# Products of the modulation moved ahead, sums kept in PSUM, and the first and last blocks of the feed-forward part reordered, in a one-core diffusion block

## The chip, the cores and the metric

The kernel runs on one core of a Trainium2 chip. The metric is the device time of one execution in microseconds (us). In the code and the views PE is TensorE, PEld its weight loads, DVE is VectorE, ACT ScalarE, POOL GpSimd and SP SyncE, whose queue issues most DMAs.

## The reference

One layer of a block over 1024 latent tokens (a 16 by 64 grid) of width 1024, with 256 context tokens beside. Cut to what matters:

```python
sh1, sc1, g1, sh2, sc2, g2 = split(silu(c) @ mod_w + mod_b, 6)
h = rms_norm(x, norm1_g) * (1 + sc1) + sh1
z_f, z_x, z_y, z_g = split(h @ w_in)                # 512 | 1024 | 1024 | 2 x 1024
f = real(fft2(z_f, per group of 128, ortho)) @ w_fourier
r = (lru_scans(z_x) * gelu(z_y)) @ w_lru_out
g_f, g_r = split(sigmoid(z_g))
x = x + g1 * ((g_f * f + g_r * r) @ w_o)
h2 = rms_norm(x, norm2_g) * (1 + sc2) + sh2
gate, val = split(dwconv3x3(h2 @ ffn_w_up), 2)      # 2 x 2816 channels
x = x + g2 * ((gelu(gate) * val) @ ffn_w_down)
return rms_norm(x, final_g)
```

All is fp32.

## The kernel before

Every matrix product is made in three: each fp32 operand is split into a high part (a copy rounded to fp32r, mostly by ScalarE, L131) and a low part (the difference, by VectorE or GpSimd, L138), and TensorE adds high x high, high x low and low x high in PSUM (`mm3`, L183 to L194). So each operand needs two instructions on other engines before TensorE can read it. Buffers in SBUF are slots of 4 KB per partition, handed out first in, first out by an allocator (`Slots`): a tile that gets a slot, and the DMA that fills it, waits until the last use of the slot before is over. No scheduler reorders anything: each engine runs its instructions in the order of the Python code, and several queues of thunks (`between` lists, `tasks`, `todo`) place the work of one chain between the matmuls of another.

The stages, with their time in the profile:

- To 370: norm, context, input projections, the two scans of the recurrence.
- `lru_out` (L855), 370 to 494: for j = 4 to 11, 48 matmuls into one bank pair, then the product with the gate (L885). Weights are loaded and split ahead by `use`.
- `fourier` (L922), 494 to 696. `fold` (L893) makes sums and differences of a channel block on GpSimd (L899) and VectorE (L903 to L913). `transform` (L947) and `project` (L962) are the two matmul steps on the folded data. `gate(j)` (L984) runs 48 matmuls of the gate's projection and calls the thunks of its `between` list after the matmul numbers given there. `merge` (L1215) joins even and odd parts of block j from PSUM, multiplies by the gate `sf[j]` and adds `self.m[j]`, the recurrent branch.
- `out_proj` (L1276), 696 to 785. `post` (L1295) multiplies by the g1 row and adds the residual.
- `ffn` (L1627), 785 to 1268: 22 blocks n of 256 channels. A block is seven products i = 0 to 6 (`up_product`, L1545, 12 matmuls each), in the manner of Strassen; `up_split` makes the parts of a product's weights (ScalarE and GpSimd), `up_join` (L1571) adds the last term on VectorE to the bank of gate ("g") or value ("v"), `up_conv` prepares the 3x3 convolution, and `taps` (L1606) does its taps on VectorE. L1661 adds two side columns on GpSimd, which value's taps need.
- `down` (L1796), 1268 to the end: seven products p, in the order 1, 2, 6, 7, 5, 4, 3, of 11 steps i of 12 matmuls. `down_sums` (L1743), `down_hi`, `down_lo` make the operands; `tasks` holds the work on finished banks, two tasks a step. Rows come out in eight tiles of 128: tiles 4 to 7 are normed by `norm` (L1825) from `tasks`, tiles 0 to 3 after the last product.

The modulation rows are made aside: `mod` (L328) multiplies 128 rows of `mod_w`, loaded by SyncE (L349), by a column of silu(c) and adds them up on VectorE (L336 for the first of eight, L338 for the others), 32 products in the order shift 2, scale 2, g1, g2. `mod_finish` (L352) counts down and then sums over the partitions, for shift and scale by transposes on TensorE (L431) and a reduction on VectorE (L432).

```python
L876  if j == 11 and i % 6 == 5:
L877      sl.free(ph[i // 6], pl[i // 6])
L878      if i == 5 or i > 20:
L879          self.mod(2 if i == 5 else 3)
L1223 nc.vector.tensor_tensor(f[:, 0:H], od, e, op=OP.add)        # od: PSUM
L1225 nc.vector.tensor_tensor(f, f, sf[j], op=OP.mult)
L1226 nc.vector.tensor_tensor(f, self.m[j], f, op=OP.add)
```

Of the kernel before, what the change touches and what calls it, by code (L numbers as in the profile page):

```python
# [112 lines left out]
class K:  # L113
# [741 lines left out]
    def lru_out(self):  # L855
# [66 lines left out]
    def fourier(self):  # L922
# [146 lines left out]
        for j in range(1, 5):  # L1069
# [3 lines left out]
            if j < 4:  # L1073
                at += [*((i, self.mod) for i in (4, 13, 22, 31, 40)),
# [201 lines left out]
    def out_proj(self):  # L1276
# [197 lines left out]
        for kp in range(4):  # L1474
            low("T3", kp, st[kp][:, 0], "pool")
            sl.free(st.pop(kp))
            if kp == 1:
                self.up_split(0, 5)
        for kp in range(4):
            low("T4", kp, f0[kp][:, 1], "pool")  # L1480
            sl.free(f0.pop(kp))
# [145 lines left out]
    def ffn(self):  # L1627
# [4 lines left out]
        todo = deque([(0, 6), (1, 4), (1, 5), (1, 6)])  # L1632
        self.down_plan()
        for n in range(NP):
# [4 lines left out]
            for m, i in [(n, 0), (n - 1, 6)] + [(n, i) for i in range(1, 6)]:  # L1639
                if m >= 0 and not (n < 2 and (i < 4 and m == n or n == 0 and i == 4)):  # L1640
                    if todo:
                        self.up_split(*todo.popleft())
# [395 lines left out]
```

## Time and profile before

| | |
|---|---|
| time, median of 3 runs | 1506.07 us (1505.95 to 1506.21) |
| profiled execution, its own time | 1508.81 us |
| its span, first to last instruction | 1507.0 us |
| mean granted TensorE clock | 0.972 of full speed |
| TensorE busy | 1397.0 us (93%), 6333 matmuls |
| VectorE busy | 1146.8 us (76%), 1330 instructions |
| ScalarE busy | 694.1 us (46%) |
| GpSimd busy | 642.3 us (43%) |
| chain that ended last, by engine | PE 39%, DVE 10%, POOL 3%, issue 3% |
| bytes moved | 155.21 MB, 103 GB/s |

TensorE is the busiest engine, and its share is the mean over stages of different kinds. The profile is read by stage: where TensorE is busy less than the whole stretch, its waits name the engine and the line that released it. A wait is put down to what came last. A granted clock below 1.00 tells that matmuls of that stretch took longer for the same work. Times in a timeline count from the start of the span.

### The profile page before, as it was taken

To read this page: it belongs to the slowest core of one execution; us is meant where nothing else is said; L and a number is where in the kernel's file an instruction comes from. 1 tells how busy PE (TensorE), PEld (TensorE's weight loads), DVE (VectorE), ACT (ScalarE), POOL (GpSimd) and SP (SyncE) were. 2 spreads that over 40 slices of the span, in tenths; PEclk is the share of its full clock that TensorE was granted. 3 is DMA by queue.
4 is the path that set the end of the run, shared out by engine and by line. 5 is a ranking of instruction groups with operands and counts; after the bars stand their busy time and mean duration, and the time that the engine had idled before them with its cause. 6 is when DMAs were issued, how large, how long until landed. Compare 5 with 4: busy or idle time off the path is not lost.

```text
span 1507.0 us, 17062 instructions
## 1 busy us (share of the span) xinstructions
PE 1397.0 (93%) x6333; PEld 1126.6 (75%) x6333; DVE 1146.8 (76%) x1330; ACT 694.1 (46%) x1006; POOL 642.3 (43%) x460
## 2 busy tenths in 40 slices
PE   5999999998999689988998699999999999999994
PEld 3788888877888578877876477777777777788883
DVE  5768768767113987577566699999999998998696
ACT  6566677755010112343235355545545555545461
POOL 2221121122001443268033999999999996200000
PEclk9999999999999899999998799999999999999997
DMA  9310110101113445322431122122222108741642
GB/s 373 110 36 22 50 35 22 63 28 42 43 48 114 168 147 168 122 85 83 140 112 53 32 85 73 62 76 85 84 84 84 62 37 315 292 147 57 234 136 112
DMA packets 52788, 155.21 MB, mean 103 GB/s; under 512 B 5781, under 2 KB 10192, under 8 KB 52704
## 3 DMA queue, kind: packets, MB, share of 16 engines
q1 hardware_dynamic: 51264, 151.76, 29.0%
q10 hardware_dynamic: 1184, 2.11, 0.5%
q8 instruction: 50, 0.82, 0.2%
q14 instruction: 34, 0.28, 0.1%
q0 software_dynamic: 256, 0.25, 0.1%
HBM read 131.29 MB, written 22.81 MB: 102 GB/s over the span
## 4 chain that ended last, share of the span: by engine, by line
PE 39%; DVE 10%; POOL 3%; issue 3%; ACT 2%; DMA 1%; POOLq 0%; SPq 0%; DVEq 0%; ACTq 0%
PE ug L1556 16%; PE uv L1556 12%; PE dn L1836 6%; PE big L194 5%; DVE s L138 3%; POOL s L138 2%; ACT uv L131 1%; DVE s L1225 1%; DVE s L1828 1%; DMA s<-G 1%; ACT s L131 1%; DVE s L1757 0%; PE big L1212 0%; DVE s L1754 0%; ACT s L1341 0%
## 5 line engine op out<-in xcount | busy, mean ns | idle before, releaser
L194 PE MATMUL big<-s,s 128*128 128x512 f32 (+2 forms) x2352 | 561.5, 397 | 8.4 <-DVE s L138 5.6
L194 PEld LDWEIGHTS big<-s,s 128*128 128x128 f32 (+2 forms) x2352 | 440.4, 190 | 114.7 <-DVE s L138 7.0
L138 POOL TENSOR_TENSOR s<-s,s 128x512 fp32r<-128x512 f32 (+1 forms) x225 | 341.5, 1536 | 206.9 <-ACT s L131 132.0
L131 ACT ACTIVATE s<-s 128x512 fp32r<-128x512 f32 (+2 forms) x406 | 266.3, 698 | 237.4 <-DVE mid L912 62.8
L1556 PE MATMUL ug<-s,s 128*128 128x512 f32 x1056 | 264.4, 398 | 17.5 <-ACT uv L131 13.4
L1556 PEld LDWEIGHTS ug<-s,s 128*128 128x128 f32 x1056 | 198.1, 189 | 72.2 <-ACT uv L131 22.0
L138 DVE TENSOR_TENSOR s<-s,s 128x512 fp32r<-128x512 f32 (+3 forms) x213 | 189.9, 923 | 75.1 <-ACT s L131 53.7
L1606 DVE SCALAR_TENSOR_TENSOR s<-ug,rest,s 128x945 f32<-128x945 f32 (+2 forms) x176 | 215.0, 1221 | 9.2 <-ACT s L1585 3.8
L1836 PE MATMUL dn<-s,s 128*128 128x512 f32 x924 | 216.5, 396 | 4.2 <-DVE s L138 4.1
L1556 PE MATMUL uv<-s,s 128*128 128x512 f32 x792 | 202.1, 404 | 17.6 <-POOL s L138 6.7
L1836 PEld LDWEIGHTS dn<-s,s 128*128 128x128 f32 x924 | 174.2, 189 | 46.2 <-DVE s L138 5.7
L1606 DVE SCALAR_TENSOR_TENSOR s<-uv,rest,s 128x945 f32<-128x945 f32 (+2 forms) x155 | 189.5, 1223 | 13.5 <-POOL s L1661 9.6
L1556 PEld LDWEIGHTS uv<-s,s 128*128 128x128 f32 x792 | 152.9, 194 | 55.8 <-POOL s L138 7.9
L782 POOL TENSOR_TENSOR s<-s,s 128x1280 f32<-128x1280 f32 x8 | 25.2, 3150 | 190.1 <-ACT s L778 190.1
L899 POOL TENSOR_TENSOR s<-s,s 128x1024 f32<-128x1024 f32 x8 | 22.2, 2780 | 126.2 <-PE big L194 120.6
L131 ACT ACTIVATE p<-uv 128x512 f32<-128x512 f32 x22 | 13.2, 599 | 103.5 <-PE uv L1556 99.8
L745 DVE SCALAR_TENSOR_TENSOR s<-big,par,s 128x1023 f32<-128x1023 f32 (+1 forms) x24 | 30.8, 1282 | 34.2 <-ACT s L742 33.6
L885 DVE TENSOR_TENSOR s<-big,s 128x1024 f32<-128x1024 f32 x8 | 9.8, 1223 | 61.1 <-PE big L194 61.1
L1504 POOL TENSOR_TENSOR s<-s,s 128x512 f32<-128x512 f32 x22 | 28.5, 1295 | 64.6 <-DMA s<-in_ffn_w_up_b_dram 64.6
L1661 POOL TENSOR_TENSOR s<-s,m 128x504 f32<-128x504 f32 (+1 forms) x42 | 45.5, 1104 | 23.7 <-ACT m L1602 23.7
L1616 POOL TENSOR_TENSOR s<-s,s 128x1024 f32<-128x1024 f32 x22 | 53.7, 2440 | 2.9 <-DVE s L1606 2.9
L777 ACT ACTIVATE s<-big,rest 128x1024 f32<-128x1024 f32 x32 | 35.7, 1117 | 24.7 <-PE big L194 17.8
(233 smaller groups left out, 1500.4 us busy)
## 6 DMA issues: line engine op xcount, KB each, us to landing
s<-in_mod_w_dram SPq DMA_DIRECT2D x48, 512.0 KB, 4.6
s<-in_ffn_w_up_b_dram SPq DMA_DIRECT2D x44, 512.0 KB, 4.2
s<-in_w_in_b_dram SPq DMA_DIRECT2D x32, 512.0 KB, 4.4
s<-G SPq DMA_DIRECT2D x55, 256.0 KB, 3.9
G<-s SPq DMA_DIRECT2D x22, 512.0 KB, 2.6
s<-in_ffn_w_down_dram SPq DMA_DIRECT2D x22, 512.0 KB, 7.3
s<-in_x_dram SPq DMA_DIRECT2D x16, 512.0 KB, 5.3
s<-G SPq DMA_DIRECT2D x11, 512.0 KB, 8.4
```

What stands on the lines that cost most here:

```text
L131: self.nc.scalar.activation(out, in_, AF.Copy)
L138: (self.nc.vector if eng == "dve" else self.nc.gpsimd).tensor_tensor(out, a, b, op=OP.subtract)
L194: return [lambda x=x: nc.tensor.matmul(x[0], x[1], x[2], start=x[3], stop=x[4]) for x in calls]
L745: nc.vector.scalar_tensor_tensor(u[:, lo:hi], z[:, lo + s:hi + s], tap[t], u[:, lo:hi], op0=OP.mult, op1=OP.add)
L777: nc.scalar.activation(lat, ps, AF.Sigmoid, bias=col)
L782: nc.gpsimd.tensor_tensor(i, i, u, op=OP.mult)
L1504: p.tensor_tensor(u["x"][:, L], rg[:, L], rv[:, L], op=OP.subtract)
L1556: nc.tensor.matmul(o, x, y, start=first, stop=k == 3 and m == 2, skip_group_check=not fresh)
L1606: nc.vector.scalar_tensor_tensor(o, i, w, o, op0=OP.mult, op1=OP.add))
L1616: nc.gpsimd.tensor_tensor(u["ga"], u["ga"], u["va"], op=OP.mult)
L1661: self.nc.gpsimd.tensor_tensor(o, o, m, op=OP.add)
L1836: nc.tensor.matmul(bank[j], x, z, start=first and m == 0, stop=end and m == 2, skip_group_check=not check)
```

## The change

1. `lru_out`: for j = 4 to 10 `mod(1)` is called after matmuls 5, 21 and 37, and `mod_finish` after each matmul from j = 5 on; at j = 11 one call of `mod` is left. In the Fourier stage `gate(0)` makes no call any more, and the gates 1 to 3 make two each, not five.
2. `merge`: the copy, difference, sum and product are written to the PSUM tile itself, and only the last addition writes SBUF. In `post` of `out_proj` the product is written in place too.
3. The FFN's start: the lows of "T4" are made earlier, the splits of (0,5), (1,4), (0,6) come directly behind those of "T3", and the three products run one after the other; then value's join and convolution of block 0, and then the splits of (1,5) and (1,6).
4. `down`: right halves of the second weight rows are multiplied by the g2 row before product 3. The residual of tiles 0 to 3, with what is already known of the right half, is copied by ScalarE into the banks X, and product 3 adds onto it. Tiles 4 to 7 are normed together behind the last lows; tiles 0 to 3 are normed by pairs, in half rows, each half with its own output DMA.

```diff
@@ lru_out
                     f()
+                    if j < 11 and i in (5, 21, 37):
+                        self.mod(1)
+                    if j > 4:
+                        self.mod_finish()
                     if j == 11 and i % 6 == 5:
                         sl.free(ph[i // 6], pl[i // 6])
-                        if i == 5 or i > 20:
-                            self.mod(2 if i == 5 else 3)
+                        if i == 5:
+                            self.mod(2)
@@ fourier
-        gate(0, [(8, lambda: step(1, 2)), (17, lambda: transform(0)), (20, lambda: step(1)), (34, lambda: transform(1)),
-                 *((i, self.mod) for i in (0, 3, 24, 32, 41))])
+        gate(0, [(8, lambda: step(1, 2)), (17, lambda: transform(0)), (20, lambda: step(1)), (34, lambda: transform(1))])
@@
-                at += [*((i, self.mod) for i in (4, 13, 22, 31, 40)),
+                at += [*((i, self.mod) for i in (22, 40)),
@@ merge
-            nc.vector.tensor_copy(f[:, H:H + 1], eb[:, Q:Q + 1])
-            nc.vector.tensor_tensor(f[:, 0:H], od, e, op=OP.add)
-            nc.vector.tensor_tensor(rev(f[:, H + 1:]), e[:, 1:], od[:, 1:], op=OP.subtract)
-            nc.vector.tensor_tensor(f, f, sf[j], op=OP.mult)
-            nc.vector.tensor_tensor(f, self.m[j], f, op=OP.add)
+            nc.vector.tensor_copy(ps[:, H:H + 1], eb[:, Q:Q + 1])
+            nc.vector.tensor_tensor(rev(ps[:, H + 1:]), e[:, 1:], od[:, 1:], op=OP.subtract)
+            nc.vector.tensor_tensor(od, od, e, op=OP.add)
+            nc.vector.tensor_tensor(ps, ps, sf[j], op=OP.mult)
+            nc.vector.tensor_tensor(f, ps, self.m[j], op=OP.add)
@@ ffn
-        todo = deque([(0, 6), (1, 4), (1, 5), (1, 6)])
+        todo = deque([(1, 5), (1, 6)])
@@
+                if n == 0 and i == 5:
+                    self.up_product(0, 5)
+                    self.up_product(1, 4)
+                    self.up_product(0, 6)
+                    self.taps(0, "gt", 8)
+                    self.up_join(0, "v")
+                    self.up_conv(0, "v")
+                    while todo:
+                        self.up_split(*todo.popleft())
+                elif m > 0 and not (n == 1 and i < 5):
@@ down_sums, p == 3
             v.tensor_tensor(x[:, L], x[:, L], x[:, R], op=OP.subtract)
+            v.tensor_tensor(o[:, R], o[:, R], self.g2row[:, R], op=OP.mult)
@@ down, p == 3 and i == 7
+                    v.tensor_tensor(ss[:, 4:8], q[:, 4:8, 0], q[:, 4:8, 1], op=OP.add)
+                    r47 = self.rstd(ss[:, 4:8])()
                     for j in range(4):
...
+                        norm(4 + j, r47[:, j:j + 1])
@@ down, tasks of p == 5
-                    def c1(j=j):
-                        v.tensor_tensor(y[j][:, H[0]], y[j][:, H[0]], c11[j], op=OP.add)
+                    def c1(j=j, b=X[j]):
                         v.tensor_tensor(y[j][:, H[1]], y[j][:, H[1]], at(u, j), op=OP.add)
-                        square(j, 0, j)
+                        self.copy("act", b, y[j][:, H[1]])
@@ down, end
-                v.tensor_tensor(r, X[j], self.g2row[:, H[1]], op=OP.mult)
-                v.tensor_tensor(y[j][:, H[1]], y[j][:, H[1]], r, op=OP.add)
-                square(j, 1, j)
-            if j:
-                norm(j - 1)
+            nc.scalar.activation(temp(j), X[j], AF.Square, accum_out=sq[:, 2 * j + 1:2 * j + 2])
+            if j % 2:
+                v.tensor_tensor(ss[:, j - 1:j + 1], q[:, j - 1:j + 1, 0], q[:, j - 1:j + 1, 1], op=OP.add)
+                r = self.rstd(ss[:, j - 1:j + 1])()
+                for t in (j - 1, j):
+                    for d, x in ((1, X[t]), (0, y[t][:, H[0]])):
+                        v.scalar_tensor_tensor(y[t][:, H[d]], x, r[:, t - j + 1:t - j + 2], fg[:, H[d]], op0=OP.mult, op1=OP.mult)
```

VectorE in `lru_out`, blocks j = 5 to 7, before: a block's product with its gate (L885), then the lows of the coming weights (L138).

```order
L885 TENSOR_TENSOR s_2458<-big,s_2458 128x1024
L138 TENSOR_TENSOR s_2909<-s_2856,s_2908 128x1024
L138 TENSOR_TENSOR s_2966<-s_2912,s_2965 128x1024
L885 TENSOR_TENSOR s_2597<-big,s_2597 128x1024
L138 TENSOR_TENSOR s_3022<-s_2969,s_3021 128x1024
L138 TENSOR_TENSOR s_3079<-s_3025,s_3078 128x1024
L885 TENSOR_TENSOR s_2648<-big,s_2648 128x1024
```

Between two L885 stand two lows and nothing else. The same place with the change (L885 is now L889):

```order
L338 SCALAR_TENSOR_TENSOR s_2752<-s_2790,s,s_2752 128x1024
L338 SCALAR_TENSOR_TENSOR s_2752<-s_2874,s,s_2752 128x1024
L338 SCALAR_TENSOR_TENSOR s_2752<-s_2893,s,s_2752 128x1024
L889 TENSOR_TENSOR s_2458<-big,s_2458 128x1024
L138 TENSOR_TENSOR s_2926<-s_2864,s_2925 128x1024
L138 TENSOR_TENSOR s_2983<-s_2929,s_2982 128x1024
L338 SCALAR_TENSOR_TENSOR s_2752<-s_2912,s,s_2752 128x1024
L338 SCALAR_TENSOR_TENSOR s_2752<-s_2996,s,s_2752 128x1024
L338 SCALAR_TENSOR_TENSOR s_2752<-s_3015,s,s_2752 128x1024
L889 TENSOR_TENSOR s_2597<-big,s_2597 128x1024
```

Two or three products of the modulation now stand behind each block's lows and ahead of the next block's L889.

GpSimd at the FFN's start, before: lows (L138), the sums for block 2 (L1504 to L1508), and the two side columns (L1661).

```order
L138 TENSOR_TENSOR s_5761<-s_5354,s_5760 128x512
L138 TENSOR_TENSOR s_5761<-s_5371,s_5760 128x512
L138 TENSOR_TENSOR s_5908<-s_5501,s_5908 128x512
L1504 TENSOR_TENSOR s_5938<-s_5904,s_5906 128x512
L1506 TENSOR_TENSOR s_5906<-s_5906 128x512
L1508 TENSOR_TENSOR s_5938<-s_5906,s_5938 128x512
L138 TENSOR_TENSOR s_5942<-s_5904,s_5942 128x512
L138 TENSOR_TENSOR s_5945<-s_5539,s_5945 128x512
L138 TENSOR_TENSOR s_5960<-s_5906,s_5960 128x512
L1661 TENSOR_TENSOR s_5963<-s_5963,m 128x8x63
L1661 TENSOR_TENSOR s_5963<-s_5963,m 128x7x63
```

Behind the lows of (0,6) (s_5908) come the sums, three lows and the side columns. With the change (L1507 to L1511 are the sums, L1672 the side columns; s_5868, s_5871 and s_5874 are lows of (0,5), (1,4) and (0,6), s_5967 and s_5970 those of (1,5) and (1,6)):

```order
L138 TENSOR_TENSOR s_5868<-s_5509,s_5868 128x512
L138 TENSOR_TENSOR s_5871<-s_5539,s_5871 128x512
L138 TENSOR_TENSOR s_5874<-s_5501,s_5874 128x512
L138 TENSOR_TENSOR s_5967<-s_5561,s_5967 128x512
L138 TENSOR_TENSOR s_5970<-s_5541,s_5970 128x512
L1507 TENSOR_TENSOR s_5977<-s_5910,s_5912 128x512
L1509 TENSOR_TENSOR s_5912<-s_5912 128x512
L1511 TENSOR_TENSOR s_5977<-s_5912,s_5977 128x512
L138 TENSOR_TENSOR s_5981<-s_5910,s_5981 128x512
L138 TENSOR_TENSOR s_5984<-s_5912,s_5984 128x512
L1672 TENSOR_TENSOR s_5961<-s_5961,m 128x8x63
L1672 TENSOR_TENSOR s_5961<-s_5961,m 128x7x63
```

The three splits now stand one behind the other, and the lows of (1,5) and (1,6) moved in front of the sums, so that seven steps stand between the low of (0,6) and the side columns.

VectorE ahead of the last matmuls, before: two norms of tiles 4 to 7 (L1828 ends one), then the last two lows (L138).

```order
L1828 SCALAR_TENSOR_TENSOR s_10396<-s_10396,r_10800,s_10340 128x1024
L1826 TENSOR_SCALAR ss_9091<-sq 128x1
L453 TENSOR_SCALAR ss_9091<-ss_9091 128x1
L454 RECIPROCAL r_10811<-t_10812 128x1
L456 TENSOR_SCALAR t_10812<-r_10811,ss_9091 128x1
L457 TENSOR_SCALAR t_10812<-t_10812 128x1
L458 TENSOR_SCALAR r_10811<-r_10811,t_10812 128x1
L1828 SCALAR_TENSOR_TENSOR s_10422<-s_10422,r_10811,s_10340 128x1024
L138 TENSOR_TENSOR s_10793<-s_10748,s_10793 128x512
L138 TENSOR_TENSOR s_10794<-s_9484,s_10794 128x512
```

The lows stand last. With the change (L1890 to L463 are the small steps for four tiles at once, L1837 the scalings):

```order
L138 TENSOR_TENSOR s_10786<-s_10761,s_10786 128x512
L138 TENSOR_TENSOR s_10787<-s_9484,s_10787 128x512
L1890 TENSOR_TENSOR ss_9091<-sq 128x4
L453 TENSOR_SCALAR ss_9091<-ss_9091 128x4
L454 RECIPROCAL r_10807<-t_10808 128x4
L460 TENSOR_TENSOR t_10808<-r_10807 128x4
L461 TENSOR_TENSOR t_10808<-t_10808,ss_9091 128x4
L462 TENSOR_SCALAR t_10808<-t_10808 128x4
L463 TENSOR_TENSOR r_10807<-r_10807,t_10808 128x4
L1837 SCALAR_TENSOR_TENSOR s_10357<-s_10357,r_10807,s_10348 128x1024
```

The last lows now stand ahead of all norms.

## Rows read from the trace of the kernel before

**Rows 1.** Busy time by stage: us, then each engine busy (instructions), PEclk, DMA share, GB/s.

```profile
370.00:494.00 124.00, 124.00 (x531) 100.21 (x530) 29.23 (x22) 12.77 (x13) 6.00 (x2) 0.99 0.25 80
494.00:532.00 38.00, 26.56 (x121) 22.20 (x120) 36.12 (x61) 7.83 (x12) 18.50 (x7) 0.78 0.39 134
...
655.00:696.00 41.00, 31.95 (x164) 26.97 (x163) 40.14 (x37) 18.36 (x34) 35.04 (x15) 0.88 0.13 39
...
1480.00:1491.00 11.00, 10.57 (x38) 8.19 (x38) 4.78 (x11) 1.63 (x5) 0.00 (x0) 0.84 0.08 34
```

**Rows 2.** Timeline of TensorE, Fourier blocks: start, us, operation [idle before <-releaser].

```profile
513.04 1.09 PE L431 MATMUL sm<-ident,s 128*128 128x128 f32 x4 [7.83 <-DVE s L338]
...
515.63 4.93 PE L979 MATMUL big<-s,s 128*128 128x256 f32 x28
...
542.97 3.05 PE L979 MATMUL big<-s,s 128*128 128x256 f32 x24
...
570.24 3.04 PE L979 MATMUL big<-s,s 128*128 128x256 f32 x24
...
589.39 3.08 PE L979 MATMUL big<-s,s 128*128 128x256 f32 x24
```

**Rows 3.** Groups of instructions of VectorE, 494 to 700: busy, mean ns, idle before.

```profile
L338 DVE SCALAR_TENSOR_TENSOR s<-s,s,s 128x1024 f32<-128x1024 f32 x25 | 38.6, 1544 | 0.4
```

**Rows 4.** Groups of instructions of VectorE, 370 to 490.

```profile
L138 DVE TENSOR_TENSOR s<-s,s 128x1024 fp32r<-128x1024 f32 x10 | 12.2, 1219 | 32.3 <-ACT s L131 21.5 <-issue 10.8
L885 DVE TENSOR_TENSOR s<-big,s 128x1024 f32<-128x1024 f32 x7 | 8.6, 1225 | 61.1 <-PE big L194 61.1
```

**Rows 5.** DMA issues of the page: count, KB each, us to landing.

```profile
s<-in_mod_w_dram SPq DMA_DIRECT2D x48, 512.0 KB, 4.6
```

**Rows 6.** Waits of TensorE, 490 to 710: us in total, times, longest.

```profile
PE big L1212 <- DVE s L1224: 8.3, 4, 3.1
```

**Rows 7.** Groups of instructions of VectorE, 494 to 700, the merges.

```profile
L1225 DVE TENSOR_TENSOR s<-s,s 128x1024 f32<-128x1024 f32 x7 | 15.5, 2209 | 0.2
L1226 DVE TENSOR_TENSOR s<-s,s 128x1024 f32<-128x1024 f32 x7 | 14.6, 2086 | 0.2
...
L1223 DVE TENSOR_TENSOR s<-big,even 128x512 f32<-128x512 f32 x7 | 4.7, 677 | 0.0
```

**Rows 8.** Timeline of VectorE, first FFN blocks.

```profile
823.10 0.70 DVE L1574 TENSOR_TENSOR ug<-ug,p 128x512 f32<-128x512 f32 x1 [4.38 <-PE ug L1556]
...
847.82 6.29 DVE L1606 SCALAR_TENSOR_TENSOR s<-uv,rest,s 128x960 f32<-128x960 f32 x5 [9.55 <-POOL s L1661]
```

**Rows 9.** Timeline of TensorE, first FFN blocks.

```profile
828.17 1.22 PE L1556 MATMUL uv<-s,s 128*128 128x512 f32 x2 [5.18 <-ACT s L131]
...
838.32 5.21 PE L1556 MATMUL uv<-s,s 128*128 128x512 f32 x12 [4.69 <-DVE uv L1574]
...
855.35 4.64 PE L1556 MATMUL uv<-s,s 128*128 128x512 f32 x10 [6.58 <-POOL s L138]
...
862.72 2.92 PE L1556 MATMUL uv<-s,s 128*128 128x512 f32 x12
```

**Rows 10.** Timeline of GpSimd, first FFN blocks.

```profile
838.09 1.28 POOL L1504 TENSOR_TENSOR s<-s,s 128x512 f32<-128x512 f32 x1
...
845.62 2.17 POOL L1661 TENSOR_TENSOR s<-s,m 128x504 f32<-128x504 f32 x2
```

**Rows 11.** Timeline of TensorE, the end.

```profile
1480.00 10.57 PE L1836 MATMUL dn<-s,s 128*128 128x512 f32 x38 [3.33 <-DVE s L138]
```

**Rows 12.** Timeline of VectorE, the end.

```profile
1478.66 1.29 DVE L138 TENSOR_TENSOR s<-s,s 128x512 fp32r<-128x512 f32 x2
...
1489.89 1.28 DVE L1828 SCALAR_TENSOR_TENSOR s<-s,r,s 128x1024 f32<-128x1024 f32 x1
...
1494.54 1.29 DVE L1828 SCALAR_TENSOR_TENSOR s<-s,r,s 128x1024 f32<-128x1024 f32 x1
...
1501.97 1.28 DVE L1828 SCALAR_TENSOR_TENSOR s<-s,r,s 128x1024 f32<-128x1024 f32 x1
```

More of the change, by code (lines that the diff above doesn't have):

```diff
@@ L1296, in post @@
             n = xn[t] = sl.get([128, 1024], any_=True)
-            nc.vector.tensor_tensor(n, ps, self.g1row, op=OP.mult)
-            nc.vector.tensor_tensor(x[t], n, x[t], op=OP.add)
+            nc.vector.tensor_tensor(ps, ps, self.g1row, op=OP.mult)
+            nc.vector.tensor_tensor(x[t], ps, x[t], op=OP.add)
             nc.scalar.activation(n, x[t], AF.Square, accum_out=ss[:, t:t + 1])
@@ L1462, in out_proj @@
                     put("B22", q, st[q][:, 1])
+                for q in range(4):
+                    low("T4", q, f0[q][:, 1], "pool")
+                    sl.free(f0.pop(q))
             for i in (1, 3):
@@ L1476, in out_proj @@
             sl.free(st.pop(kp))
[L1477 to L1481, printed above, removed]
+        for n, i in ((0, 5), (1, 4), (0, 6)):
+            self.up_split(n, i)
     PRODUCTS = (("A11", "B11", "a0"), ("S2", "T2", "a1"), ("A12", "B21", "a0"), ("S1", "T1", "v1"),
@@ L1658, in ffn @@
                 elif i == 6:
-                    self.up_conv(n - 1, "v")
+                    if n > 1:
+                        self.up_conv(n - 1, "v")
                     for o, m in self.U[n - 1]["vr"]:
@@ L1670, in ffn @@
                     self.taps(n - 1, "vt", 8)
-            if n == 0:
-                self.taps(0, "gt", 8)
-            if n < last:
+            if 0 < n < last:
                 self.up_join(n, "v")
@@ L1823, in square, with norm @@
             nc.scalar.activation(temp(j), y[t][:, H[d]], AF.Square, accum_out=sq[:, 2 * t + d:2 * t + d + 1])
-        def norm(t):
-            v.tensor_scalar(ss[:, t:t + 1], sq[:, 2 * t:2 * t + 1], sq[:, 2 * t + 1:2 * t + 2], None, op0=OP.add)
-            r = self.rstd(ss[:, t:t + 1])()
+        def norm(t, r):
             v.scalar_tensor_tensor(y[t], y[t], r, fg, op0=OP.mult, op1=OP.mult)
@@ L1868, in down @@
                 self.down_until(self.down_lo, s + (3 if p != 3 else 4))
-                if p == 5 and i in (5, 6, 7, 8):
-                    fetch(i - 5)
+                if p == 5 and i in (3, 4, 5, 6):
+                    fetch(i - 3)
                 if p == 4 and i in (0, 1, 2, 3):
                     fetch(4 + i)
-                for _ in range(2 if i else 0):
+                for _ in range((3 if p == 4 else 2) if i else 0):
                     if tasks:
@@ L1880, in down @@
                         tasks.popleft()()
+                    v.tensor_tensor(ss[:, 4:8], q[:, 4:8, 0], q[:, 4:8, 1], op=OP.add)
+                    r47 = self.rstd(ss[:, 4:8])()
                     for j in range(4):
-                        for q in range(4):
-                            mm(s + q, X, [j], False, q == 3)
-                    for q in range(4):
-                        sl.free(*self.ready.pop(s + q))
+                        norm(4 + j, r47[:, j:j + 1])
+                    for j in range(4):
+                        for z in range(4):
+                            mm(s + z, X, [j], False, z == 3)
+                    for z in range(4):
+                        sl.free(*self.ready.pop(s + z))
                     break
@@ L1910, in down @@
                 for j in range(4):
-                    tasks.append(lambda j=j: v.tensor_tensor(at(u, j), at(u, j), self.g2row[:, H[1]], op=OP.mult))
+                    tasks.append(lambda j=j: v.tensor_tensor(y[j][:, H[0]], y[j][:, H[0]], c11[j], op=OP.add))
+                for j in range(4):
+                    tasks.append(lambda j=j: square(j, 0, j))
             elif p == 5:
@@ L1916, in down, with c12 @@
                 for j in range(4):
+                    def c12(j=j, b=X[j]):
+                        v.tensor_tensor(at(u, j), b, at(u, j), op=OP.add)
+                        v.tensor_tensor(at(u, j), at(u, j), self.g2row[:, H[1]], op=OP.mult)
                     def c22(j=j, b=X[j]):
```

19 lines of the change are left out of this document (7 added, 12 removed).

## The prediction

> **What bounds the kernel now.** I read the stage table first, then the waits in the stages where TensorE is not full. TensorE is the bound almost everywhere: from 370 to 494 it is busy for the whole 124 us while VectorE is busy for 29 [rows 1]. It falls back in four places, and the change touches all four: (a) the Fourier blocks, 26.56 us busy of the 38 from 494 on, at a granted clock of 0.78; (b) the merges from 655 to 696, 31.95 of 41 at 0.88; (c) the start of the FFN, around 840, by three waits that part D names; (d) the end, where only 10.57 us of matmuls come after 1480, at 0.84 [rows 1]. In each of them other engines set the time, so each part of the change is costed by what is late in its own stage.
>
> The bound for "no change" is 0.2%, 3 us: the runs shown agree within 0.3 us, and a measurement of a newly built kernel can't tell much less than that.
>
> **A, modulation products.** In (a) TensorE's longest stop is 7.83 us, at a transpose that waits for VectorE's product L338 [rows 2]. The projections that start at 515.63, 542.97, 570.24 and 589.39 show the price of one round: 27.3, 27.3, then 19.15 us once it runs freely [rows 2]. Lost are 7.8 + 8.2 + 8.1 = 24 us. VectorE does 25 products by L338 there at a mean of 1.54 us [rows 3], between the folds that the transforms depend on. The change moves 16 products ahead, some 25 us of VectorE, and the transposes of the finished ones, which wait for them, too. These cost TensorE up to 1.09 us a group [rows 2], about 1.5 in all, in either place. So -22.
> What is paid for it, between 370 and 494: 16 products of about 1.3 us on a VectorE that stands idle 61 us behind TensorE's blocks [rows 4], and 16 loads of 512 KB, 4.6 us each from issue to landing [rows 5]. These are on SyncE's queue, ahead of some weight loads, and they take buffers: counted through the program's allocator, 0 to 3 slots stay free there where 3 to 6 did, so a weight's load comes out later. It has a whole block, 124 us by 531 matmuls by 48 or 11.2 us, to hide in. I take +1; the ends are 0 and rival 3. A = -21, from -24 to -15 (GpSimd's part of the folds as the next limit).
>
> **B, merges in PSUM.** TensorE waits four times for the second reader of the bank, L1224, 8.3 us in all [rows 6]; the stage has 9 us of idle time and some 2 of lower clock to lose [rows 1]. A merge has two operations of 1024 columns whose operands all lie in SBUF, 2.21 and 2.09 us, while those of half that width from PSUM take 0.68 [rows 7]; GpSimd is busy beside both. One of 1024 columns from PSUM takes 1.22 where GpSimd rests [rows 4]. An operation that reads and writes PSUM in place, L1574, takes 0.70 for 512 [rows 8]. So I take 1.25 for each of the two, between 1.22 and 2.2, since the rows with PSUM beside a busy GpSimd are the nearest; a merge falls from 5.8 to about 3.9 us. Against it: the bank is held until the last addition instead of L1224, some 2.5 us longer within a merge. With the banks there are, the seventh block's matmuls then end near 685.6 instead of 696.3. B = -10, from -12 to -4.
> The Trainium skill, "VectorE: DVE Perf Modes", section "Rules for kernel authors", says of elementwise work on a matmul's output to accept the 1x rate from PSUM, or to copy to SBUF first when many operations follow. By that rule this part goes the wrong way, and B would be 0 or above. The rows of this stage speak against it, since it is the SBUF operations that take over 2 us.
>
> **C, out_proj.** Two operations per row tile write elsewhere, none is added, and the multiplication's target in PSUM costs what L1574 shows [rows 8]. A shorter addition ends where TensorE isn't waiting. 0, within 1 us.
>
> **D, the first FFN blocks.** Now TensorE stops 5.18 us at (0,5) for ScalarE, 4.69 at (0,6) for join(0,v) and 6.58 in (1,5) for GpSimd's lows; (1,6) starts at 862.72 [rows 9]. In the new order (0,5), (1,4) and (0,6) follow each other with no join between: I put their ends at 835.5, 838.7 and 841.5. That much is won. But (1,5) and (1,6) still need their splits, which now come behind conv(0,v): ScalarE is free for them at about 845.2. GpSimd has then, in this order, two lows, three sums for block 2, two lows more, and only behind these seven the additions L1672 that v's taps wait for. At 1.28 us a step, and 2.17 for the two additions [rows 10], they end near 845.2 + 8.9 + 2.2 = 856.3. Now VectorE takes these taps up at 847.82, after waiting 9.55 us [rows 8]. The taps, two joins and what lies between then run to 866.4, and (1,6) starts there: +3.7. A stop of about 10 us lies ahead of it, and the 12 matmuls behind such a stop take 5.21 instead of 2.92 us [rows 9]: +2.3. D = +6, from -6 (rival 1) to +8. The steady blocks behind it stay as they are.
>
> **E, the end.** TensorE waits 3.33 us at 1480.00 for L138 [rows 11]: the last lows run from 1478.66 to 1479.95 [rows 12] behind four norms. What a norm costs is seen on the last row, which has no sum in front: 1501.97 - 1494.54 less the 4.65 of a whole row is 2.8 us [rows 12]. These 11 us move behind the lows. Put in front are 11 multiplications and four that come later than they did, at 0.6 us from one to the next [rows 12], 9 to 9.5 us. So the last lows end at 1478.3, TensorE's stop falls to about 1.5 us, and its last 38 matmuls, 10.57 us now [rows 11], run at the 0.23 of a full clock (124 by 531 [rows 1]), 8.8 us: end at 1487.2 instead of 1490.6. Behind it, a row now costs 4.65 us of serial steps, 1489.89 to 1494.54 [rows 12]; two sums a row, 0.7 each, vanish, and the chain of small steps is paid for two rows at once. Norms of rows 4 to 7 until 1485, first pair 1489.4, second 1493.8. The output behind the last scaling took 1507.0 - 1503.25 = 3.75 us; end near 1497.4. E = -9, from -11 to -4.
>
> **Sum:** -21 - 10 + 0 + 6 - 9 = -34 us. The stages lie one behind the other, so the terms add. The profiled execution took 1508.81 (span 1507.0), 2.7 over the median of 1506.07; set on the median, 1472.
>
> **Rivals.**
> 1. *The FFN start gains.* If the splits come out sooner than I count, or L1672 by 850, two of the three waits go [rows 9]: D = -6, time 1460. For: 16.4 us of waits stand there to be had. Against: GpSimd's order. 0.18.
> 2. *Half of A stays.* GpSimd's folds are late as soon as VectorE is not, the two rounds fall to 24 and not to 19 us: A = -10, time 1483. For: TensorE's free round at 570.24 lies where fewer folds are left. Against: the stop at 513.04 is put down to VectorE alone. 0.09.
> 3. *The weights come late before the Fourier stage.* If a load can't start until the block in front has given back its slot, TensorE stands for load, conversion and low, 4.6 + 1.0 + 1.2 = 6.8 us a block [rows 1, 4, 5] (1.0 is ScalarE's 12.77 us by 13). It decides from the fifth block on, since 5 x 6.8 eats the 34 us; with seven the time is 1472 + 47 = 1519, slower. For: 0 to 3 free slots. Against: one slot a block is enough. 0.04.
> 4. *PSUM operations are no faster.* Beside a busy GpSimd those of 1024 columns take as long as from SBUF, or the longer hold eats the gain: B = 0, time 1482. For: the hold, 2.5 us a merge. Against: 0.68 for 512 in that very stage [rows 7]. By the skill's rule above it would be the likeliest; the rows leave it 0.08.
>
> **How the numbers follow.** The forecast has 0.59, the rivals 0.39, two of the bad ones at once 0.02 (about 1493). The forecast's own terms spread it from 1465 to 1480. The range takes in rival 1 with 2 us below, and rivals 2 and 4 with 4 above: 1458 to 1487. It leaves out rival 3, the double case, and the outer part of the others. Faster by more than 3 us holds in all cases but rival 3 and a mishap of its size: 0.95; same 0.01, slower 0.04.
>
> **What would show it.** A: no wait of TensorE for L338, and rounds of 19 to 20 us from the first on. B: the two operations of 1024 columns at 1.2 to 1.3 us, and TensorE's waits in the merges below 2 us in all. D: an idle time of 8 to 10 us ahead of (1,6), put down to VectorE's join, with v's taps waiting for L1672. E: matmuls ending 3 us sooner, and the second pair's scalings 4.4 us behind the first's. The forecast is wrong in its reasons if (1,6) starts no later than now, counted from the FFN's first product, or if TensorE stops between 370 and 494 for a weight.

## The result: 1481.5 us, and the profile after

The changed kernel takes 1481.51 us (median of 4, 1480.06 to 1482.07) against 1506.14 us for the kernel before on the same chip: a ratio of 0.9834, 95% interval 0.9817 to 0.9851. That is 24.6 us less; forecast were 34, with a range that reaches from 1458 to 1487 us. The profiled execution of before took 1508.81, that of after 1480.06, so the two traces stand 28.7 us apart (spans 1507.0 and 1478.3), some 4 more than the medians do. What follows about stages is read from the two traces, so the terms of the table below are together some 4 us too large.

Four places that both traces have cut the difference into the terms of the prediction:

| up to | before, us | after, us | ahead by | this term | forecast |
|---|---|---|---|---|---|
| the seventh projection starts [rows 2] | 589.39 | 575.20 | 14.2 | A: -14.2 | -21 |
| the last merge's matmuls are done | 696.34 | 671.34 | 25.0 | B: -10.8 | -10 |
| product (2,2), first of the steady blocks | 869.10 | 849.84 | 19.3 | C, D: +5.7 | +6 |
| the end of the span | 1507.0 | 1478.3 | 28.7 | E: -9.4 | -9 |

The first cut isn't quite fair to A: ahead of it the changed kernel has four matmuls of the g1 row's broadcast (L419) that the kernel before has behind it. Cut at the first matmul of the merges instead (651.83 before, 636.10 after), A is -15.7 and B -9.3. So B, D and E came near their forecasts in size, and A is 5 to 7 us short. TensorE's timeline of the Fourier stage shows where, to be read beside [rows 2]:

```profile
510.59 5.00 PE L983 MATMUL big<-s,s 128*128 128x256 f32 x27 [2.45 <-DVE s L962]
...
531.73 3.05 PE L983 MATMUL big<-s,s 128*128 128x256 f32 x24
...
536.28 2.60 PE L194 MATMUL big<-s,s 128*128 128x512 f32 x10 [1.27 <-ACT s L1000]
...
553.57 0.70 PE L419 MATMUL sm<-s,ones 128*128 128x512 f32 x2 [2.36 <-DVE s L962]
...
555.52 3.03 PE L983 MATMUL big<-s,s 128*128 128x256 f32 x24
...
575.20 3.05 PE L983 MATMUL big<-s,s 128*128 128x256 f32 x24
```

The stop of 7.83 us is gone, but the rounds are 21.1, 23.8 and 19.7 us, not 19 to 20 from the first on. Three stops are left, 6.1 us together, and two of them are for L962, the lows of a transform on VectorE. These lows come late because the folds in front of them do. VectorE and GpSimd in the first gate of the changed kernel, from two timelines:

```profile
500.90 2.90 DVE L909 TENSOR_TENSOR fo<-s 128x511 f32<-128x511 f32 x1
503.84 2.48 DVE L910 TENSOR_TENSOR s<-fe 128x256 f32<-128x256 f32 x1
506.25 2.62 DVE L911 TENSOR_TENSOR s<-fe 128x256 f32<-128x256 f32 x1
508.79 0.41 DVE L912 TENSOR_TENSOR s<-fo 128x255 f32<-128x255 f32 x1
```

```profile
500.80 5.24 POOL L138 TENSOR_TENSOR s<-s,s 128x1024 fp32r<-128x1024 f32 x2 [9.95 <-ACT s L131]
506.00 2.58 POOL L903 TENSOR_TENSOR s<-s,s 128x1024 f32<-128x1024 f32 x1
```

Three operations of VectorE, which took 0.69, 0.42 and 0.42 us in the fold ahead of this one, take 2.9, 2.5 and 2.6. GpSimd runs three instructions in this stretch, of about 2.6 us each, and each operation of VectorE ends within 0.6 us of the end of one of GpSimd's. The next, with GpSimd at rest, takes 0.41.

Before the Fourier stage the moved products cost nearly nothing. The row of the stage table that answers to the first of [rows 1]:

```profile
370.00:494.00 124.00, 124.00 (x536) 100.45 (x536) 52.62 (x46) 13.34 (x13) 5.75 (x2) 0.98 0.44 145
```

VectorE has gone from 29 to 53 us busy, TensorE is still busy for all 124, and TensorE waits for nothing in this stretch.

The merges of the changed kernel, groups of instructions of VectorE from 640 to 678, answer to [rows 7]:

```profile
L1228 DVE TENSOR_TENSOR big<-big,s 128x1024 f32<-128x1024 f32 x8 | 9.9, 1232 | 0.3
L1229 DVE TENSOR_TENSOR s<-big,s 128x1024 f32<-128x1024 f32 x8 | 9.8, 1224 | 0.3
...
L138 DVE TENSOR_TENSOR s<-s,s 128x1024 fp32r<-128x1024 f32 x3 | 5.2, 1744 | 0.0
```

The two wide operations take 1.23 and 1.22 us where they took 2.21 and 2.09, though GpSimd is as busy beside them. Only L138, the low of a weight of w_o, still has all its operands in SBUF, and it takes 1.74 on the mean. The whole stretch of the merges, first before and then after, with the columns of [rows 1]:

```profile
651.83:696.34 44.51, 35.47 (x186) 30.23 (x184) 41.45 (x37) 20.49 (x36) 36.40 (x17) 0.88 0.13 39
636.10:671.34 35.24, 30.85 (x185) 26.71 (x184) 31.30 (x37) 20.75 (x36) 28.40 (x17) 1.00 0.15 51
```

Of the 9.3 us between them TensorE's waiting gives 4.7 (9.0 to 4.4) and the matmuls themselves 4.6 (35.5 to 30.9): the granted clock of the stretch went from 0.88 to 1.00.

The first FFN blocks, TensorE's timeline first, to be read beside [rows 8 to 10]:

```profile
803.61 1.22 PE L1559 MATMUL uv<-s,s 128*128 128x512 f32 x2 [5.18 <-ACT s L131]
...
841.58 4.81 PE L1559 MATMUL uv<-s,s 128*128 128x512 f32 x12 [9.10 <-DVE uv L1577]
846.23 2.95 PE L1559 MATMUL ug<-s,s 128*128 128x512 f32 x12
849.84 3.04 PE L1559 MATMUL ug<-s,s 128*128 128x512 f32 x12 [0.67 <-ACT uv L131]
```

The last of these is product (2,2); before it stood here:

```profile
869.10 3.04 PE L1556 MATMUL ug<-s,s 128*128 128x512 f32 x12 [0.67 <-ACT uv L131]
```

VectorE, then GpSimd:

```profile
831.66 6.30 DVE L1609 SCALAR_TENSOR_TENSOR s<-uv,rest,s 128x960 f32<-128x960 f32 x5 [13.91 <-POOL s L1672]
```

```profile
827.00 2.51 POOL L138 TENSOR_TENSOR s<-s,s 128x512 fp32r<-128x512 f32 x2
829.47 2.16 POOL L1672 TENSOR_TENSOR s<-s,m 128x504 f32<-128x504 f32 x2
```

(1,6) starts at 841.58, behind one stop of 9.10 us for the join, and its 12 matmuls take 4.81 us. The taps of v waited 13.91 us for the side columns.

The end, TensorE and then VectorE, beside [rows 11, 12]:

```profile
1459.27 0.96 PE L1845 MATMUL dn<-s,s 128*128 128x512 f32 x3 [1.41 <-DVE s L138]
1460.47 9.06 PE L1845 MATMUL dn<-s,s 128*128 128x512 f32 x38 [0.24 <-DVE s L138]
```

```profile
1457.92 2.50 DVE L138 TENSOR_TENSOR s<-s,s 128x512 fp32r<-128x512 f32 x4
...
1468.31 0.75 DVE L1965 SCALAR_TENSOR_TENSOR s<-dn,r,s 128x512 f32<-128x512 f32 x1
...
1472.53 0.75 DVE L1965 SCALAR_TENSOR_TENSOR s<-dn,r,s 128x512 f32<-128x512 f32 x1
```

The stop for the last lows is 1.41 + 0.24 us instead of 3.33, the last 38 matmuls take 9.06 instead of 10.57, and the two pairs of rows follow each other in 4.2 us where a single row took 4.65.

### The profile page after: what moved, and what is told of

It is laid out like the page before. It is cut to its first block, busy times and chain, and to the rows that moved or that the text cites. A ratio compares the mean times of both kernels' runs of the same rounds, so it can differ in the third digit from the quotient of the medians.

```text
span 1478.3 us, 17075 instructions
## 1 busy us (share of the span) xinstructions
PE 1390.1 (94%) x6333; PEld 1120.2 (76%) x6333; DVE 1133.8 (77%) x1314; ACT 695.6 (47%) x1005; POOL 628.3 (42%) x460
## 4 chain that ended last, share of the span: by engine, by line
PE 47%; DVE 8%; issue 3%; ACT 2%; POOL 2%; DMA 1%; SPq 0%; DVEq 0%; POOLq 0%; ACTq 0%
PE ug L1559 16%; PE uv L1559 11%; PE big L194 9%; PE dn L1845 9%; DVE s L138 2%; POOL s L138 1%; ACT uv L131 1%; PE big L983 1%; DVE s L1609 1%; DMA s<-in_ffn_w_down_dram 1%; DVE big L1228 1%; DVE s L1780 0%; DVE s L1779 0%; DVE s L1837 0%; DVE s L1965 0%
## 5 line engine op out<-in xcount | busy, mean ns | idle before, releaser
L138 POOL TENSOR_TENSOR s<-s,s 128x512 fp32r<-128x512 f32 (+1 forms) x225 | 329.5, 1484 | 204.3 <-ACT s L131 127.1
L138 DVE TENSOR_TENSOR s<-s,s 128x512 fp32r<-128x512 f32 (+3 forms) x213 | 190.8, 928 | 73.1 <-ACT s L131 62.7
L1507 POOL TENSOR_TENSOR s<-s,s 128x512 f32<-128x512 f32 x22 | 28.5, 1296 | 68.3 <-DMA s<-in_ffn_w_up_b_dram 68.3
L1672 POOL TENSOR_TENSOR s<-s,m 128x504 f32<-128x504 f32 (+1 forms) x42 | 45.5, 1105 | 25.5 <-ACT m L1605 25.5
L338 DVE SCALAR_TENSOR_TENSOR s<-s,s,s 128x1024 f32<-128x1024 f32 x28 | 42.1, 1503 | 14.8 <-DMA s<-in_mod_w_dram 14.5
```

What stands on the lines that cost most here:

```text
L138: (self.nc.vector if eng == "dve" else self.nc.gpsimd).tensor_tensor(out, a, b, op=OP.subtract)
L338: nc.vector.scalar_tensor_tensor(self.acc, t, col, self.acc, op0=OP.mult, op1=OP.add)
L1507: p.tensor_tensor(u["x"][:, L], rg[:, L], rv[:, L], op=OP.subtract)
L1672: self.nc.gpsimd.tensor_tensor(o, o, m, op=OP.add)
```

## The experiments

Two questions were open: why A is short, and whether the parts are worth alone what they show together.

**Each part alone.** `e1_products_ahead` is the kernel before with item 1 of the change, `e2_merge_psum` with `merge` of item 2, `e3_tail` with item 4; their diffs are those pieces of the change. `e4_old_ffn_start` is the changed kernel without item 3.

> The kernel before with part A alone. Theory (the parts add, and A is worth what the trace of the changed kernel shows up to the last projection, 589.39 against 575.20): 14 to 15 us faster than before, about 1491.5, with rounds of 20 to 24 us between projections and waits for L958's counterpart (the lows of the transforms) in the place of the one for L338. Rival (half of the moved work is paid back later, in the merges, which then start with less VectorE behind them): 8 to 11 us, about 1496. Rival (my forecast): 21 us, about 1485.

Measured: 1493.04 us, ratio to before 0.9919 (0.9904 to 0.9933), 12 to 13.5 us faster. Nearest is the first theory, a little short of it; 21 us are out. The waits of TensorE from 490 to 710 in this kernel:

```profile
PE big L1215 <- DVE s L1227: 8.3, 4, 3.1
PE big L194 <- ACT s L1000: 2.8, 1, 2.8
PE big L983 <- DVE s L962: 2.4, 1, 2.4
```

The waits for L338 and for the columns of L432 are gone, the one for L962 is there, and the merges wait exactly as before, 8.3 us.

> The kernel before with part B alone. Theory (the two wide operations escape the waiting beside GpSimd): merges of 4.0 to 4.2 us as in the changed kernel, 9 to 11 us faster, about 1496. Rival (B's gain in the changed kernel comes in part from a later start of GpSimd's lows, due to A): 4 to 7 us.

Measured: 1503.68 us, ratio 0.9980 (0.9970 to 0.9991): 3 us, less than either range, where the same edit is worth 9.3 to 10.8 in the changed kernel's trace. All eight merges ran at the new rate. But timelines of VectorE, GpSimd and TensorE show this between the third and the fourth:

```profile
668.63 8.47 DVE L138 TENSOR_TENSOR s<-s,s 128x1024 fp32r<-128x1024 f32 x1
```

```profile
661.33 14.69 POOL L138 TENSOR_TENSOR s<-s,s 128x512 fp32r<-128x512 f32 x9 [1.51 <-ACT s L131]
```

```profile
681.31 1.83 PE L1212 MATMUL big<-s,s 126*128 126x512 f32 x4 [6.28 <-DVE big L1222]
```

One low of w_o, an instruction of 1.22 us where GpSimd rests [rows 4], takes 8.47. It ends at 677.10, about 1 us after nine GpSimd instructions without a gap have ended (661.33 + 14.69 = 676.02). TensorE then waits 6.28 us for the merge behind it. To tell this from a loss of another kind, `e9_merge_alone_no_dve_low` takes the four lows of w_o that VectorE makes, this one among them, to GpSimd:

```diff
-            q.append(self.w_rows(a["w_o"][0], k, None, "pool" if k % 2 else "dve"))
+            q.append(self.w_rows(a["w_o"][0], k, None, "pool"))
```

> Part B alone, as e2_merge_psum, with the lows of all eight blocks of w_o on GpSimd, so that no VectorE instruction in the merges has all its operands in SBUF. Theory (B alone lost 6 us at one such low of VectorE, 8.47 us long beside nine GpSimd instructions without a gap): that wait is gone, and B alone is worth 8 to 10 us, about 1497. Rival (GpSimd's four added lows make it late for the products of out_proj): 3 us or less, as e2_merge_psum.

Measured: 1496.67 us, ratio 0.9932 (0.9917 to 0.9947), 10.3 us faster. The theory holds: with no VectorE instruction on SBUF operands alone left there, TensorE's waits in the merges are one of 2.5 us, and B together with the moved lows is worth what B is in the changed kernel. What the moved lows would give without B was not run, so the 10.3 us are those of the two edits; on top of a kernel that has B (`e14_both` to `e15_both_no_dve_low`, below) the same move gave nothing clear.

```profile
PE big L1212 <- DVE big L1222: 2.5, 1, 2.5
```

> The kernel before with part E alone. Theory: 9 to 10 us faster, about 1496.5, the matmuls ending some 1.5 to 2 us sooner and the serial part behind them 7 to 8 us shorter. Rival (the gain in the changed kernel is the run-to-run difference of profiled executions): 5 us.

Measured: 1495.78 us, ratio 0.9937 (0.9922 to 0.9952), 9.5 to 10.7 us faster: the theory. TensorE's last stops are those of the changed kernel:

```profile
1475.47 0.97 PE L1836 MATMUL dn<-s,s 128*128 128x512 f32 x3 [1.44 <-DVE s L138]
1476.68 8.98 PE L1836 MATMUL dn<-s,s 128*128 128x512 f32 x38 [0.23 <-DVE s L138]
```

> The changed kernel with part D undone, the order of the first FFN blocks as before. Theory (D costs 5 to 6 us, by the additions of the side columns that stand behind seven other steps of GpSimd): about 1476, 5 to 6 us faster than the changed kernel. Rival (the difference of 5.7 us between the end of the merges and the steady blocks is from part C, or from the later state of GpSimd): same as the changed kernel, 1481.

Measured: 1474.02 us, ratio 0.9792 (0.9776 to 0.9808). With 0.9834 for the changed kernel that is 6.3 us faster: the new order of the FFN's start costs what was forecast for it. The steady blocks begin at 843.67, not at 849.84:

```profile
843.67 1.65 PE L1559 MATMUL ug<-s,s 128*128 128x512 f32 x6 [0.67 <-ACT uv L131]
```

By the ratios the parts alone are worth -12.2, -3.0, -9.5 and +6.3, together -18.4, while the whole change gives -25.0; with e9 in the place of e2 (-10.2) they give -25.6, with the moved lows in it. As far as these runs tell, the parts add once B is not spoiled by that single instruction.

**What holds the FFN's start.** `e5_columns_first` moves the side columns of block 0 ahead:

```diff
                     self.up_conv(0, "v")
+                    for o, m in self.U[0]["vr"]:
+                        self.nc.gpsimd.tensor_tensor(o, o, m, op=OP.add)
                     while todo:
```

> The changed kernel, with GpSimd's two additions L1672 for block 0 put directly behind the convolution of value, ahead of the lows of (1,5) and (1,6), the sums and the lows of block 2. Theory (these additions, behind seven steps, hold up the taps of v and so (1,6)): v's taps start some 8 us sooner, TensorE's wait of 9.1 us for the join falls below 2, and the time is 7 to 10 us shorter, about 1473. Rival (ScalarE's split of (1,5) and not GpSimd's order sets it): under 3 us, 1479 or more.

Measured: 1479.02 us, ratio 0.9818 (0.9803 to 0.9832), 2.4 us below the changed kernel and not clear of it. What was expected of the taps came, what was expected of the time didn't. Timelines of VectorE and ScalarE:

```profile
821.66 6.29 DVE L1609 SCALAR_TENSOR_TENSOR s<-uv,rest,s 128x960 f32<-128x960 f32 x5 [4.08 <-POOL s L1651]
...
838.90 0.70 DVE L1577 TENSOR_TENSOR uv<-uv,u 128x512 f32<-128x512 f32 x1 [7.99 <-ACT u L131]
```

```profile
834.29 0.63 ACT L131 ACTIVATE s<-s 128x512 fp32r<-128x512 f32 x1 [4.64 <-POOL s L1525]
...
838.28 0.59 ACT L131 ACTIVATE u<-uv 128x512 f32<-128x512 f32 x1
```

The taps start 10 us sooner, and then the join of (1,v) waits 8 us for ScalarE's copy u, so that TensorE's wait for the join is 7.83 us, not below 2. ScalarE stands at a split of block 2 that waits for GpSimd's L1525. Neither theory had this: it is ScalarE, but its queue and not the split of (1,5).

`e10_columns_and_14` also brings (1,4) ahead:

```diff
+            if kp == 2:
+                self.up_split(1, 4)
...
         self.up_product(0, 4)
+        self.up_product(1, 4)
```

> As e5_columns_first, and also the split and the product of (1,4) moved ahead to right behind (0,4), where TensorE waits 5.2 us for ScalarE. Theory: (1,4) fills that wait, (0,6) ends 3 to 4 us sooner, and the time falls by another 3 to 4 us, to about 1469.5. Rival (the taps of the gate, 10 us on VectorE, end too late for it to matter): same as e5_columns_first within 1 us.

Measured: 1477.55 us, ratio 0.9810 (0.9793 to 0.9826), 3.6 us below the changed kernel; its interval overlaps with that of the changed kernel and with that of e5. The wait for ScalarE ahead of (0,5) fell from 5.2 to 3.3 us only, (0,6) ended at 815.99 where e5 has 816.77, and the later wait for the join is still 6.26 us.

`e12_sums_early` starts from e10 and moves the three sums of block 2 into GpSimd's idle time, and the gelu of block 0 behind the join:

```diff
                     self.up_product(0, 6)
+                    self.up_sums(2)
                     self.taps(0, "gt", 8)
...
-                    if n == 1 and i == 0:
-                        self.up_sums(2)
...
-                    self.gelu(n - 1)
+                    if n > 1:
+                        self.gelu(n - 1)
...
                 self.up_join(n, "v")
+            if n == 1:
+                self.gelu(0)
```

> As e10_columns_and_14, with GpSimd's three sums for block 2 moved from behind the lows of (1,5) and (1,6) to behind the split of (0,6), where GpSimd rests for 9 us, and the gelu of block 0 moved on ScalarE to behind the join of (1,v). Theory (in e5 and e10 the join of (1,v) waited 8 us for ScalarE's copy u, which stood behind splits of block 2 that waited for GpSimd's sums, so what bounds this stage is GpSimd's line of work from 819 to 842): the copy comes 5 to 6 us sooner, TensorE's wait of 6.3 us falls below 2, and the time is 4 to 6 us below e10, about 1472.5. Rival (the sums of block 2 find no free buffer so early, and GpSimd's order stalls there): same as e10 or slower.

Measured: 1470.33 us, ratio 0.9758 (0.9739 to 0.9778): 11.4 us below the changed kernel, clear of it. Against e4, with the old order, it is 3.7 us lower by the medians and 5.1 by the ratios, whose intervals just overlap. The join now waits 1.82 us for u, and TensorE 3.85 for the join, where below 2 was expected. TensorE and VectorE:

```profile
832.01 5.49 PE L1562 MATMUL uv<-s,s 128*128 128x512 f32 x12 [3.85 <-DVE uv L1580]
```

```profile
831.25 0.70 DVE L1580 TENSOR_TENSOR uv<-uv,u 128x512 f32<-128x512 f32 x1 [1.82 <-ACT u L131]
```

So the new order of products no longer costs anything that shows, and is likely the better one, once GpSimd's work is put into the gaps that it leaves. The sums and the gelu were not tried apart, but the traces of e10 and e12 show a share for each: the split of block 2 that ScalarE waits for ahead of u gets its operand at 828.98 instead of 833.48, 4.5 us sooner, and the gelu with its table load, 2.25 us, no longer stands between that split and u (837.50 in e10, 830.64 in e12).

**What holds the Fourier stage.** `e6_fold_lows_dve` takes GpSimd's lows from beside the folds:

```diff
-        self.sub("pool", lo, r, hi.bitcast(F32))
+        self.sub("dve", lo, r, hi.bitcast(F32))
...
-            q.append(self.w_cols(win, GF + 128 * j, lo="pool" if j else "dve"))
+            q.append(self.w_cols(win, GF + 128 * j, lo="pool" if j > 4 else "dve"))
```

> The changed kernel, with the lows of the folds and of the first five gates' weights moved from GpSimd to VectorE. Theory (A fell short because VectorE's folds, all with two operands in SBUF, stand still while GpSimd works): the folds' slow instructions of 2.4 to 2.9 us go back to 0.4 to 0.7, TensorE's waits of 6 us between 500 and 560 mostly vanish, 4 to 7 us faster, about 1476. Rival (VectorE is short of time by its own work): no gain or a loss of up to 4 us, since VectorE gets 12 more instructions of 1.2 us.

Measured: 1483.17 us, ratio 0.9845 (0.9830 to 0.9859): no gain. But the trace holds both theories, one after the other. TensorE's timeline, and one row of VectorE's:

```profile
535.65 3.04 PE L983 MATMUL big<-s,s 128*128 128x256 f32 x24
...
547.99 0.71 PE L419 MATMUL sm<-s,ones 128*128 128x512 f32 x2 [3.98 <-DVE s L962]
...
562.72 2.08 PE L955 MATMUL sm<-tc__3455,wraw 128*128 128x128 f32 x8 [5.16 <-DVE s L420]
```

```profile
555.46 1.23 DVE L138 TENSOR_TENSOR s<-s,s 128x1024 fp32r<-128x1024 f32 x1 [6.04 <-ACT s L131]
```

The fourth projection starts at 535.65; in the changed kernel it started at 542.87, 7.2 us later, so the folds were held by GpSimd. Their operations show it too: L909 from 496 to 570, in the changed kernel and then in e6:

```profile
L909 DVE TENSOR_TENSOR fo<-s 128x511 f32<-128x511 f32 x8 | 9.9, 1234 | 0.0
L909 DVE TENSOR_TENSOR fo<-s 128x511 f32<-128x511 f32 x8 | 5.5, 683 | 0.0
```

Then VectorE stands 6.04 us at the low of a gate's weight, whose high part waits on ScalarE for a buffer that the projection before gives back, and all that follows in VectorE's queue stands with it. `e13_fold_lows_only` therefore keeps the second edit of e6 out:

> The changed kernel, with the lows of the folds alone on VectorE; those of the gates' weights stay on GpSimd. Theory (in e6_fold_lows_dve the projections came 7 us sooner, by taking GpSimd's work from beside the folds, until VectorE stood 6 us behind the low of a gate's weight that waited for a buffer): the first four projections come 4 to 6 us sooner and that wait is gone, 3 to 5 us faster than the changed kernel, about 1477.5. Rival (what is gained at the folds is lost at the first broadcast of g1, which waits for VectorE's queue): same within 1.5 us.

Measured: 1477.60 us, ratio 0.9808 (0.9790 to 0.9827), 3.9 us below the changed kernel. The intervals overlap a little, so this is likely rather than shown by the times; its trace has the first four projections 2.0 to 4.0 us sooner, where 4 to 6 were expected, and no stop of 6 us. The fourth:

```profile
538.92 3.04 PE L983 MATMUL big<-s,s 128*128 128x256 f32 x24
```

**Both together**, e12 with the edit of e13, and the same with the edit of e9:

> The reordered FFN start of e12_sums_early together with the folds' lows on VectorE of e13_fold_lows_only, on top of the changed kernel. Theory (the two lie in stages one behind the other, so the gains of 11 and 4 us add): about 1466.5, some 15 us below the changed kernel. Rival (as with the merges, an earlier stage that ends otherwise shifts the next against GpSimd's line of work): 1469 to 1471, no better than e12_sums_early.

> As e14_both, with the lows of all of w_o's blocks on GpSimd. Theory (in the changed kernel VectorE's lows in the merges take 2.3, 1.5 and 1.4 instead of 1.2 us, so little is to be had): within 1.5 us of e14_both. Rival (TensorE's waits of 2.4 and 1.5 us in the merges come from these lows): 3 to 4 us faster. Rival (GpSimd gets late with w_o for out_proj): 2 us slower or more.

Measured: 1470.38 us (ratio 0.9755, 0.9736 to 0.9774) and 1469.08 us (0.9768, 0.9754 to 0.9782). Neither is better than e12 beyond the uncertainty. The median of `e14_both` lies in its rival's range, but its four executions lie between 1464.31 and 1472.21 us, wider than those of the kernel before beside it (1502.97 to 1507.14); in the fastest, the one with a trace, the steady blocks begin 7.2 us sooner than in e12. Whether the gains add there stays open. The best version found is e12 and its two descendants, 10 to 12 us below the changed kernel and 35 to 37 below the one before, by the ratios.

## Why the prediction was right, and where it was off

The bound of 3 us for "no change" was drawn from three runs that agree within 0.3 us. Later executions of the same kernel lie between 1503.55 and 1510.43 us in one series of 13, so it was none too wide.

**A was mis-sized.** The mechanism came as put down: no wait for L338, nothing lost between 370 and 494 for a weight, transposes moved along. The step that failed is the term "-22", which took every round down to the free 19.15 us. Measured: 14.2 to 15.7 us in the trace, 12 to 13.5 alone. What stands in the place of L338 is what rival 2 named and had at 0.09, GpSimd's part of the folds; not as work that is late itself, but because VectorE's operations stand still while GpSimd works. I had the slow products of 1.54 us mean in [rows 3] in hand and read them as VectorE's own load; the same slowness sits in the folds, and that part stays when the products go. e6 shows it: 7.2 us sooner at the fourth projection with GpSimd's lows away. One of the three stops left is also the change's own doing: the broadcast of g1, L419, now falls at 553.57, into the tight rounds, and waits 2.36 us.

**B was right in size, partly by luck.** The operations take the forecast 1.25 us. But TensorE's waits in the merges are 4.4 us, not below 2. The larger, 2.43, ends with the last addition of the third merge:

```profile
652.36 1.05 PE L1215 MATMUL big<-s,s 126*128 126x512 f32 x4 [2.43 <-DVE s L1229]
```

That is the longer hold of the bank, which the prediction had named; it had expected less than 2 us of waits in all. The other, 1.53, stands behind the merge that a low of w_o on VectorE, 2.27 us long, had held up. What the waits didn't give the clock did: 4.6 of the 9.3 us are faster matmuls, where the prediction had "some 2 of lower clock" to lose; [rows 1] had more, 0.12 of 31.95 us or about 3.8. That B alone gives 3 us, and 10.3 with the four lows moved, shows how near the gain was to being lost, and that the parts added in the changed kernel was luck. The Trainium skill, "VectorE: DVE Perf Modes", section "Rules for kernel authors", would accept the rate from PSUM, or copy to SBUF first for many operations. Here, with four operations a merge and a copy, accepting the rate from PSUM was faster than going on in SBUF, by 3.0 us in e2 and, with the lows moved, by 10.3 in e9.

**C** shows a little. The last row tile's bank is now held for both operations, so the first product of the FFN waits 2.44 us for L1301 where it waited 1.09 for L1297, and starts 91.07 us behind the merges instead of 89.32. The prediction had a shorter addition end where TensorE isn't waiting. By the FFN's third product 0.4 us of it is left (100.68 against 100.31).

**D was right, by its own steps.** Between the end of the merges and (1,6) lie 166.38 us before and 170.24 after: +3.9, forecast +3.7. Counted from the FFN's first product, as the prediction's sign has it, (1,6) comes 2.1 us later (79.17 against 77.06), and from the third 3.5; the rest is what C does. The stop is 9.10 us, forecast about 10, put down to the join, with v's taps behind L1672. The 12 matmuls behind it take 4.81 us; the forecast took 5.21. e4 measures 6.3 us for the whole. What I had not seen is that L1672 was only the first of two holds: with it out of the way (e5), ScalarE's copy u was late by GpSimd's sums. The order of work on GpSimd and ScalarE as a whole sets this stage, as e12 tells.

**E was right in its sum**, at 9.4 of 9 us, and 9.5 to 10.7 alone, but two errors cancel. Counted from (2,2), the last lows end only 0.3 us sooner (610.58 against 610.85), where 1.7 was forecast. The matmuls end 1.8 us sooner, forecast 3, and 1.5 of that is that the last 38 run at a granted clock of 1.00 instead of 0.84. The serial part behind them is 7.7 us shorter (8.8 instead of 16.4), forecast 6.2, and makes up for it.

Rival 1 fell, since the start lost; rival 2 came half true, with rounds between its 24 and the free 19; rivals 3 and 4 fell with the first trace.

## What to carry to other kernels

When a wait is taken away, ask what the instructions behind it look like while the neighbour engine works: an operation that is slow by its neighbour stays slow when the queue in front of it gets shorter. Operations on a matmul's output can stay in PSUM where GpSimd is busy, but then look for the one instruction in that stretch that still reads only SBUF. And where a chain crosses three engines in program order, moving one link ahead uncovers the next: put whole pieces of work (sums of a later block, an activation that nobody waits for yet) into the idle stretches.

## What the runs showed of the hardware

A VectorE operation with all its operands in SBUF is held up by GpSimd far beyond a shared rate: 0.42 us became 2.5 beside GpSimd instructions of 2.6 us, and in `e2_merge_psum` 1.22 became 8.47 beside nine without a gap. Operations that read one operand from PSUM show nothing of it: 0.70 for 512 and 1.23 for 1024 columns in the same stretches. In the changed kernel the low at the same place of the program, beside eleven such GpSimd instructions, took 2.27 us; why VectorE got in there and not in e2 is open. The Trainium skill, "GPSIMD Engine Reference", section "Key points", states that GpSimd shares its SBUF interfaces with VectorE, with contention for VectorE instructions that have two SBUF inputs. These traces agree with it, and give the size.

The second thing is the clock behind a stop. After 9.10 us of waiting, 12 matmuls took 4.81 us instead of 2.95, at a granted clock of 0.58 on the mean of that stretch. After the 6.28 us stop in e2 four took 1.83 instead of 0.98, at 0.50, the lower of the two levels (1.2 of 2.4 GHz). But the length of the stop alone doesn't tell the price. At the first stop in the merges, 2.43 us in the changed kernel, four matmuls took 1.05 at a granted clock of 1.00; at the same place in e2 they took as long as after 6.28, at 0.50:

```profile
668.86 1.83 PE L1212 MATMUL big<-s,s 126*128 126x512 f32 x4 [2.40 <-DVE s L1226]
```

In the kernel before, 2.49 us of waiting there were followed by 0.59 of the clock for 4.2 us, and in e12 the 12 matmuls behind 3.85 us took 5.49, at 0.50, longer than behind 9.10. What else decides, these runs don't show.
